# Three modulation rows moved from the output product to the class products, sums of squares put behind rows, and u's block sums put two tiles later

## The chip, the cores and the metric

The kernel runs on one core of one Trainium2 chip. The metric is the time of the whole program in device microseconds (us), as the median of several runs. A profiled execution gives, beside its own time, a trace of every instruction; positions in that trace are told in us from the first instruction.

## What is computed

One decoder block on 512 tokens of width 1024, everything in float32. A conditioning vector gives 9 x 1024 modulation values, a shift, a scale and a gate for each of three sub-layers. The sub-layers are a SwiGLU feed-forward, a token-mixing layer and a second SwiGLU; a last RMSNorm follows. What matters here, cut from the reference:

```python
mod = silu(c) @ w_ada + b_ada            # 9 x 1024: sh1, sc1, gt1, sh2, sc2, gt2, sh3, sc3, gt3
u = modulate(rmsnorm(h, g1), sh1, sc1);  h = h + 0.5 * gt1 * swiglu(u, ...)
u = modulate(rmsnorm(h, g2), sh2, sc2);  h = h + gt2 * token_mixing(u, ...)
u = modulate(rmsnorm(h, g3), sh3, sc3);  h = h + 0.5 * gt3 * swiglu(u, ...)
return rmsnorm(h, g_final)

# token_mixing: proj = u @ w_in -> p, q, k, v, gate logits
#   pooling of p, three groups of dilated window attention, merged by their softmax denominators
merged = g_pool * (y_pool @ w_pool_branch) + g_attn * (y_attn @ w_attn_branch)
return merged @ w_out
```

## The kernel before

**Products.** Activations stand feature by token, eight tiles of 128 features by 512 tokens. Each float32 operand of a product is split into a high part (ScalarE copies it to the matmul's format: `whi`, `UH`) and a low part (VectorE subtracts: `wlo`, `UL`), and each product is three matmuls, high x high, high x low, low x high (`mm3`, lines 356 to 362). Weights come by DMA in chunks of 512 KB (`raw`), are split three or four tiles ahead of their use, and stand in a ring of seven chunks.

**Modulation rows.** The 72 rows of 128 modulation values are not made on TensorE. `bg` (line 406) does one: VectorE multiplies a 128 x 1024 chunk of `w_ada` with the broadcast condition and sums along the row (line 387, one SCALAR_TENSOR_TENSOR with an accumulator). `bg_fetch` (line 422) loads the next chunks from the SyncE queue (line 379) into the tiles of `ada_free`, at most `ada_depth` rows ahead, and a chunk's tile can be loaded again only when VectorE has read it. After the eighth row of a group `ada_fin` adds the bias and, by kind, multiplies the gain in (scale) or halves (last gate).

**The mixing layer** (`mix`, line 1247). After the projections of q, k and a part of v come the attention tiles. Work on attention is put beside the projection's matmuls by hooks: `hooks(new, ...)` returns, for a tile, what is to be recorded ahead of which of its eight contraction steps k. Step 5 always carries the attention of three stages: the value products of the unit begun two tiles earlier (`at_values`, line 1138, TensorE), the transposes of the last unit, the scores of the new one, and its maximum and exponential (`at_exp`, VectorE lines 1112 and 1114, ScalarE line 1117). The four products of the values by residue class c (loop at line 1381) write one bank each; VectorE copies it to `v23` (line 1396), and the value products read `v23` in the next tile's step 5. Two tiles of gate logits follow (`gates`), with the merge of the softmax denominators (`at_merge`) and the pooling's small products.

GpSimd computes the pooling's running means in `pool_diff` (line 1205), beside the class products.

**u's block sums** (`mix_sums`, line 969) are thirteen small steps that a later blocked product of the gate logits needs: sums and differences of quarters of u on VectorE, each 128 x 1024, and their split in high and low parts. `nxt` pops the next one where a hook calls it. The names `PH`, `YL`, `YH` and `cs` are the tiles that hold them.

**The output product** (end of `merge_out`, line 1456). Tiles m = 0 to 4 of `w_out` times the merged branches, each 512 tokens wide; behind each, VectorE adds gate x product to the residual (`H`, line 1543), ScalarE squares it, and VectorE adds the square to a running sum `acc`, the lower half of tile `AR` (`sumsq`, lines 432 to 440). `bg` is called 3, 3, 2, 2 and 1 times behind the five tiles, for rows 61 to 71. Tiles 5 to 7 follow in `out_tail` (line 519), halved by tokens; in the second half of tile 6 TensorE sums `acc` over the features (`stats_t`, line 450), and the next norm starts from that. So all eight squares of the first half must have been added by then (the last three at line 557).

Each engine works through its own instructions in the order in which they were recorded; semaphores hold an instruction until its inputs are there.

## Time and profile before

| | |
|---|---|
| median of 3 runs (995.24, 996.4, 997.64) | 996.4 us |
| the profiled execution: its own time, its span in the trace | 995.25 us, 993.5 us |
| TensorE busy | 981.3 us, 99% of the span |
| VectorE busy | 787.3 us, 79% |
| ScalarE busy | 475.3 us, 48% |
| GpSimd busy | 33.9 us, 3% |
| mean granted TensorE clock | 0.999 |

In the trace's rows PE is TensorE, PEld its weight load, DVE VectorE, ACT ScalarE, POOL GpSimd and SPq the queue of SyncE, which issues the loads. A timeline row tells start, duration, engine, line, operation, output and input, shapes, and in brackets how long the engine sat idle before it and what ended that. A row of the waits tells who waited for whom: total, times, longest. A row of the windows tells, for a stretch of time, its length and then each engine's busy time and instruction count in it. Times of VectorE rows overlap a little at their ends, so what an instruction takes in a full queue is told below by the distance of two starts.

### The profile page before, as it was taken

To read this page: it belongs to the slowest core of one execution; us is meant where nothing else is said; L and a number is where in the kernel's file an instruction comes from. 1 tells how busy PE (TensorE), PEld (TensorE's weight loads), DVE (VectorE), ACT (ScalarE), POOL (GpSimd) and SP (SyncE) were. 2 spreads that over 40 slices of the span, in tenths; PEclk is the share of its full clock that TensorE was granted. 3 is DMA by queue.
4 is the path that set the end of the run, shared out by engine and by line. 5 is a ranking of instruction groups with operands and counts; after the bars stand their busy time and mean duration, and the time that the engine had idled before them with its cause. 6 is when DMAs were issued, how large, how long until landed. Compare 5 with 4: busy or idle time off the path is not lost.

```text
span 993.5 us, 16359 instructions
## 1 busy us (share of the span) xinstructions
PE 981.3 (99%) x6686; PEld 893.9 (90%) x6686; DVE 787.3 (79%) x1091; ACT 475.3 (48%) x713; POOL 33.9 (3%) x31
## 2 busy tenths in 40 slices
PE   9999999999999999999999999899999999999997
PEld 7888998989999899787879998898899899998997
DVE  7989969889797677889768877868797776676764
ACT  6453643525435453455545552455365254352553
POOL 0000000000000000007400000000000000000002
PEclk9999999999999999999999999999999999999999
DMA  9856445455563416663133336622344134241312
GB/s 348 276 196 223 149 148 178 161 191 165 181 203 106 140 56 211 213 199 120 33 118 107 107 91 201 219 64 89 103 150 135 56 110 146 85 149 43 105 45 85
DMA packets 44876, 141.74 MB, mean 143 GB/s; under 512 B 6273, under 2 KB 9089, under 8 KB 44802
## 3 DMA queue, kind: packets, MB, share of 16 engines
q1 hardware_dynamic: 44226, 140.18, 43.5%
q8 instruction: 52, 0.85, 0.3%
q10 hardware_dynamic: 576, 0.52, 0.2%
q14 instruction: 22, 0.18, 0.1%
HBM read 135.29 MB, written 2.24 MB: 138 GB/s over the span
## 4 chain that ended last, share of the span: by engine, by line
PE 83%; DVE 8%; DMA 3%; SPq 2%; ACT 2%; issue 2%; POOL 0%; POOLq 0%; DVEq 0%; ACTq 0%
PE bank L747 13%; PE bank L748 13%; PE bank L749 13%; PE bank L360 12%; PE bank L361 12%; PE bank L362 12%; DVE wlo L329 2%; SPq L1050 1%; PE bank L1710 1%; PE bank L1712 1%; PE bank L1714 1%; DMA v<-wada 1%; DMA rt<-tr 1%; DVE k L387 1%; DVE v L387 1%
## 5 line engine op out<-in xcount | busy, mean ns | idle before, releaser
L329 DVE TENSOR_TENSOR wlo<-raw,whi 128x1024 fp32r<-128x1024 f32 (+4 forms) x162 | 172.7, 1078 | 48.7 <-ACT whi L317 48.4
L747 PE MATMUL bank<-UH,whi 128*128 128x256 f32 x640 | 177.0, 276 | 0.0
L748 PE MATMUL bank<-UL,whi 128*128 128x256 f32 x640 | 176.9, 276 | 0.0
L749 PE MATMUL bank<-UH,wlo 128*128 128x256 f32 x640 | 176.9, 276 | 0.0
L317 ACT ACTIVATE whi<-raw 128x1024 fp32r<-128x1024 f32 (+4 forms) x162 | 146.1, 920 | 57.7 <-DVE raw L261 54.8
L360 PE MATMUL bank<-HI,whi 128*128 128x512 f32 (+1 forms) x406 | 146.2, 360 | 0.0
L361 PE MATMUL bank<-HK,whi 128*128 128x512 f32 (+1 forms) x406 | 145.9, 359 | 0.0
L362 PE MATMUL bank<-HI,wlo 128*128 128x512 f32 (+1 forms) x406 | 145.8, 359 | 0.0
L329 DVE TENSOR_TENSOR wlo<-X,whi 128x1024 fp32r<-128x1024 f32 (+3 forms) x104 | 111.9, 1083 | 32.2 <-ACT whi L317 31.8
L747 PEld LDWEIGHTS bank<-UH,whi 128*128 128x128 f32 x640 | 120.1, 188 | 0.4
L749 PEld LDWEIGHTS bank<-UH,wlo 128*128 128x128 f32 x640 | 120.3, 188 | 0.0
L748 PEld LDWEIGHTS bank<-UL,whi 128*128 128x128 f32 x640 | 120.2, 188 | 0.0
L747 PE MATMUL bank<-SH,whi 128*128 128x256 f32 x408 | 112.9, 277 | 0.0
L749 PE MATMUL bank<-SH,wlo 128*128 128x256 f32 x408 | 112.8, 276 | 0.0
L748 PE MATMUL bank<-SL,whi 128*128 128x256 f32 x408 | 112.8, 276 | 0.0
L317 ACT ACTIVATE whi<-X 128x1024 fp32r<-128x1024 f32 (+3 forms) x104 | 95.7, 943 | 34.3 <-DVE X L261 33.5
L360 PE MATMUL bank<-UH,whi 128*128 128x512 f32 (+1 forms) x304 | 105.7, 348 | 0.0
L361 PE MATMUL bank<-UL,whi 128*128 128x512 f32 (+1 forms) x304 | 104.3, 343 | 0.1
L362 PE MATMUL bank<-UH,wlo 128*128 128x512 f32 (+1 forms) x304 | 104.1, 342 | 0.0
L362 PEld LDWEIGHTS bank<-HI,wlo 128*128 128x128 f32 x406 | 76.2, 188 | 11.6
L360 PEld LDWEIGHTS bank<-HI,whi 128*128 128x128 f32 x406 | 76.2, 188 | 11.5
L361 PEld LDWEIGHTS bank<-HK,whi 128*128 128x128 f32 x406 | 76.3, 188 | 11.3
(345 smaller groups left out, 1841.9 us busy)
## 6 DMA issues: line engine op xcount, KB each, us to landing
raw<-wmix SPq DMA_DIRECT2D x44, 512.0 KB, 3.8
raw<-wf1i SPq DMA_DIRECT2D x31, 512.0 KB, 5.0
raw<-wf2i SPq DMA_DIRECT2D x30, 512.0 KB, 3.7
ada<-wada SPq DMA_DIRECT2D x23, 512.0 KB, 5.6
AR<-wada SPq DMA_DIRECT2D x16, 512.0 KB, 4.4
X<-wf2i SPq DMA_DIRECT2D x14, 512.0 KB, 3.7
cs<-wada SPq DMA_DIRECT2D x12, 512.0 KB, 3.7
X<-wf1i SPq DMA_DIRECT2D x12, 512.0 KB, 4.6
```

The source lines that it names most:

```text
L317: self.nc.scalar.activation(self.hi[:, y], r[:, x], AF.Copy)
L329: self.nc.vector.tensor_tensor(self.lo[:, y], r[:, x], self.hi[:, y], op=OP.subtract)
L360: M(ps, hi, uh, start=start, stop=False)
L361: M(ps, hi, ul, start=False, stop=False)
L362: M(ps, lo, uh, start=False, stop=stop)
L387: self.nc.vector.scalar_tensor_tensor(t[:, c], t[:, c], 1.0, self.cond[:, c], op0=OP.mult, op1=OP.mult, accum_out=o)
L747: M(o, hi, uh, start=start and p == 0 and k == 0, stop=False, skip_group_check=True)
L748: M(o, hi, ul, start=False, stop=False, skip_group_check=True)
L749: M(o, lo, uh, start=False, stop=k == 3, skip_group_check=True)
L1050: nc.sync.dma_start(w[32 * o:32 * o + 32], t[32 * i:32 * i + 32])
L1710: M(b, hi, self.UH[k], start=k == 0, stop=False)
L1712: M(b, hi, self.UL[k], start=False, stop=False)
```

## The change

Three things move; nothing is computed otherwise, and TensorE's and GpSimd's instructions stand in the same order as before.

- Rows 61, 62 and 63 of the modulation go from behind tiles 0 and 1 of the output product to three hooks: class product 2 at step 6, class product 3 at step 7, and the second gate tile at step 1. Their chunks are loaded one at a time into `AR`. The output product then calls `bg` 2, 2, 2, 2 and 0 times.
- In the output product the addition of a tile's square is recorded behind that tile's rows, not ahead of them.
- The block sums start two pops later: one step stays in the tile ahead of the class products, none stands in class product 0, one in class product 1, and the others in class products 2 and 3 and the gate tiles. Two steps are merged into one pop.

```diff
@@ mix_sums
-                lambda: (hi(0), whole(x[3], 4, 0)), lambda: lo(0), lambda: sub(x[3], x[3], x[1]), lambda: hi(1),
+                lambda: (hi(0), whole(x[3], 4, 0)), lambda: lo(0), lambda: (hi(1), sub(x[3], x[3], x[1])),
                 lambda: hi(2), lambda: lo(2), lambda: lo(1)], last
@@ mix
             assert self.ada_next == 61 and not self.adat, self.ada_next
+            self.ada_free, self.ada_stop, self.ada_depth = [self.AR], 64, 1
+            self.bg_fetch()
...
-            b = self.mm_tile(hooks(g23[0], [(2, lambda: by_class(1)), (3, nxt), (7, nxt)]))
+            b = self.mm_tile(hooks(g23[0], [(2, lambda: by_class(1)), (3, nxt)]))
...
+            beside = [(1, 7, nxt), (2, 2, nxt), (2, 3, clear), (2, 6, self.bg), (2, 7, nxt), (3, 2, self.at_swap), (3, 2, nxt),
+                      (3, 3, nxt), (3, 6, nxt), (3, 7, self.bg)]
             for c in range(4):
                 mid = [lambda c=c: by_class(c + 1)] if c in (1, 2) else []
-                hk = hooks(g23[c + 1], [(2, nxt), (7, nxt)] if c < 2 else [(2, clear)], mid) if c < 3 else \
-                    hooks([], [(2, self.at_swap), (2, nxt), (3, nxt), (6, nxt)])
+                hk = hooks(g23[c + 1] if c < 3 else [], [(k, f) for n, k, f in beside if n == c], mid)
...
-            gates = [self.mm_tile(hooks([], [(5, self.at_merge), (7, nxt)]))]
+            gates = [self.mm_tile(hooks([], [(2, nxt), (5, self.at_merge), (7, nxt)]))]
...
-            gates.append(self.mm_tile({1: [nxt], 3: [nxt], 6: [pool_map, lambda: self.at_fT(self.bS[1])]}))
+            gates.append(self.mm_tile({1: [self.bg, nxt], 3: [nxt], 6: [pool_map, lambda: self.at_fT(self.bS[1])]}))
@@ merge_out
-                self.sumsq(m, self.H[m])()
-                for _ in range((3, 3, 2, 2, 1)[m]):
+                add = self.sumsq(m, self.H[m])
+                for _ in range((2, 2, 2, 2, 0)[m]):
                     self.bg()
+                add()
```

What this does to VectorE's order is seen at three places. In the rows, `v_3281` is the tile `v23`, `q_3276` the tile of the fourth block sum, `uc` the low part of the first, `k_...` and `v_...` with line 387 a row's chunk; numbers of tiles differ between the two programs.

The first place is VectorE between the maxima of class product 0 and those of class product 1. Before:

```order
L1114 TENSOR_SCALAR negmax<-st 128x2
L977 TENSOR_TENSOR YL<-UH,UL 128x1024
L1396 COPY v_3281<-bank_96 128x512
L987 TENSOR_TENSOR YH<-YL,cs 128x1024
L329 TENSOR_TENSOR wlo<-raw_66,whi 128x1024
L1152 COPY q_3274<-bank_97 128x256
```

Now (the copy to `v23` is line 1400):

```order
L1114 TENSOR_SCALAR negmax<-st 128x2
L1400 COPY v_3281<-bank_96 128x512
L329 TENSOR_TENSOR wlo<-raw_66,whi 128x1024
L1152 COPY q_3274<-bank_97 128x256
L1112 ISA prob,st<-bank_90,masks 128x256
```

The block sum ahead of the copy and the one behind it are gone; the two that stood ahead of these maxima (`PH`, lines 977 and 996) are gone too.

The second place is VectorE from the last maxima to the end of class product 3. Before:

```order
L1114 TENSOR_SCALAR negmax<-st 128x2
L1396 COPY v_3281<-bank_95 128x512
L977 TENSOR_TENSOR q_3276<-UH,UL 128x1024
L985 TENSOR_TENSOR uc<-PH,k_4494 128x1024
L1152 COPY q_3274<-bank_97 128x256
L987 TENSOR_TENSOR q_3276<-q_3276,YL 128x1024
L1396 COPY v_3281<-bank_96 128x512
L329 TENSOR_TENSOR wlo<-raw_68,whi 128x1024
```

Now:

```order
L1114 TENSOR_SCALAR negmax<-st 128x2
L387 SCALAR_TENSOR_TENSOR AR,mod<-AR,cond 128x1024
L977 TENSOR_TENSOR YL<-UH,UL 128x1024
L1400 COPY v_3281<-bank_95 128x512
L987 TENSOR_TENSOR YH<-YL,cs 128x1024
L987 TENSOR_TENSOR YL<-PH,YL 128x1024
L1152 COPY q_3274<-bank_97 128x256
L977 TENSOR_TENSOR q_3276<-UH,UL 128x1024
L387 SCALAR_TENSOR_TENSOR AR,mod<-AR,cond 128x1024
L1400 COPY v_3281<-bank_96 128x512
L329 TENSOR_TENSOR wlo<-raw_68,whi 128x1024
```

Two rows and three block sums now stand in this stretch around the two copies, and two of the steps that stood here follow later. On the SyncE queue a load of `AR` stands ahead of the two small transfers of `at_swap` and another behind them.

The third place is VectorE in the output product, from the residual of tile 1 on. Before:

```order
L1543 SCALAR_TENSOR_TENSOR H<-bank_92,mod,H 128x512
L440 TENSOR_TENSOR AR<-AR,ut 128x512
L387 SCALAR_TENSOR_TENSOR k_5496,mod<-k_5496,cond 128x1024
L387 SCALAR_TENSOR_TENSOR k_5497,mod<-k_5497,cond 128x1024
L387 SCALAR_TENSOR_TENSOR v_5498,mod<-v_5498,cond 128x1024
L329 TENSOR_TENSOR wlo<-raw_67,whi 128x1024
L1543 SCALAR_TENSOR_TENSOR H<-bank_93,mod,H 128x512
L440 TENSOR_TENSOR AR<-AR,ut 128x512
```

Now:

```order
L1547 SCALAR_TENSOR_TENSOR H<-bank_92,mod,H 128x512
L387 SCALAR_TENSOR_TENSOR v_5506,mod<-v_5506,cond 128x1024
L387 SCALAR_TENSOR_TENSOR k_5504,mod<-k_5504,cond 128x1024
L440 TENSOR_TENSOR AR<-AR,ut 128x512
L329 TENSOR_TENSOR wlo<-raw_67,whi 128x1024
L1547 SCALAR_TENSOR_TENSOR H<-bank_93,mod,H 128x512
L387 SCALAR_TENSOR_TENSOR k_5505,mod<-k_5505,cond 128x1024
L387 SCALAR_TENSOR_TENSOR v_5506,mod<-v_5506,cond 128x1024
L440 TENSOR_TENSOR AR<-AR,ut 128x512
```

The addition of the square (line 440) has changed places with the rows, and one row fewer stands in this tile; behind tile 0 one row fewer stands too, and behind tile 4 none.

## The prediction

> **What bounds the kernel now.** I read the page first, then who waited for whom on TensorE, then windows and timelines around the two waits found there. The page:

> ```profile
> span 993.5 us, 16359 instructions
> PE 981.3 (99%) x6686; PEld 893.9 (90%) x6686; DVE 787.3 (79%) x1091; ACT 475.3 (48%) x713; POOL 33.9 (3%) x31
> ```

> TensorE is idle for 993.5 - 981.3 = 12.2 us in all, and its instructions are the same in the same order after the change. So the change can gain only idle time of PE. PE's waits between 440 and 660 us (total, times, longest):

> ```profile
> PE bank L450 <- DVE AR L557: 2.6, 1, 2.6
> PE bank L1147 <- DVE v L1396: 0.9, 1, 0.9
> PE bank L460 <- DVE r L455: 0.3, 1, 0.3
> ```

> The two larger ones are the places that the change touches, and both name VectorE. First the class products, as windows (length; PE, PEld, DVE, ACT, POOL busy; clock, DMA share, GB/s):

> ```profile
> 470.00:480.00 10.00, 9.24 (x70) 7.92 (x72) 9.88 (x20) 7.29 (x15) 9.63 (x7) 1.00 0.08 27
> 480.00:505.00 25.00, 25.00 (x166) 19.89 (x163) 13.85 (x32) 10.95 (x21) 2.26 (x2) 1.00 0.19 55
> ```

> VectorE is full from 470 to 480 and has 25.00 - 13.85 = 11.15 us free from 480 to 505. Its timeline ahead of the first wait, and PE's:

> ```profile
> 462.17 1.23 DVE L329 TENSOR_TENSOR wlo<-raw,whi 128x1024 fp32r<-128x1024 f32 x1 [0.44 <-ACT whi L317]
> 463.31 1.25 DVE L996 TENSOR_TENSOR PH<-PH,cs 128x1024 f32<-128x1024 f32 x1
> 464.48 2.32 DVE L329 TENSOR_TENSOR wlo<-raw,whi 128x1024 fp32r<-128x1024 f32 x1
> ...
> 468.80 1.21 DVE L977 TENSOR_TENSOR YL<-UH,UL 128x1024 f32<-128x1024 f32 x1
> 469.94 0.68 DVE L1396 COPY v<-bank 128x512 f32<-128x512 f32 x1
> ```

> ```profile
> 470.76 1.09 PE L1147 MATMUL bank<-probT,v 128*64 128x128 f32 x16 [0.90 <-DVE v L1396]
> ...
> 479.67 1.09 PE L1147 MATMUL bank<-probT,v 128*64 128x128 f32 x16
> ...
> 488.57 1.09 PE L1147 MATMUL bank<-probT,v 128*64 128x128 f32 x16
> ...
> 496.16 1.09 PE L1147 MATMUL bank<-probT,v 128*64 128x128 f32 x16
> ```

> The value products wait for a copy that stands behind block sums in VectorE's queue. Second the output product:

> ```profile
> 608.97 0.75 DVE L1543 SCALAR_TENSOR_TENSOR H<-bank,mod,H 128x512 f32<-128x512 f32 x1 [4.60 <-PE bank L362]
> ...
> 609.64 1.22 DVE L387 SCALAR_TENSOR_TENSOR k<-k,cond 128x1024 f32<-128x1024 f32 x1
> ...
> 610.78 1.22 DVE L387 SCALAR_TENSOR_TENSOR k<-k,cond 128x1024 f32<-128x1024 f32 x1
> ...
> 614.91 0.69 DVE L440 TENSOR_TENSOR AR<-AR,ut 128x512 f32<-128x512 f32 x1 [0.70 <-ACT ut L439]
> 615.52 1.22 DVE L387 SCALAR_TENSOR_TENSOR k<-k,cond 128x1024 f32<-128x1024 f32 x1
> ...
> 618.99 1.22 DVE L329 TENSOR_TENSOR wlo<-raw,whi 128x1024 fp32r<-128x1024 f32 x1
> 620.13 0.74 DVE L1543 SCALAR_TENSOR_TENSOR H<-bank,mod,H 128x512 f32<-128x512 f32 x1
> ...
> 634.75 0.48 DVE L516 SCALAR_TENSOR_TENSOR H<-bank,mod,H 128x256 f32<-128x256 f32 x1
> ...
> 640.07 0.42 DVE L557 TENSOR_TENSOR AR<-AR,gc 128x256 f32<-128x256 f32 x1
> ```

> ```profile
> 614.66 0.39 PE L362 MATMUL bank<-v,wlo 128*128 128x512 f32 x1
> ...
> 633.94 0.28 PE L362 MATMUL bank<-v,wlo 128*128 128x256 f32 x1
> ...
> 640.54 0.71 PE L450 MATMUL bank<-ones,AR 128*128 128x128 f32 x4 [2.59 <-DVE AR L557]
> ```

> The residual of tile 2 starts at 620.13 though its bank was done at 614.66 + 0.39 = 615.05: VectorE runs five us late behind the rows, and when PE comes to sum the squares, at 640.54 - 2.59 = 637.95, the last addition ends only at 640.07 + 0.42 = 640.49. Tile 0 still found VectorE waiting for PE (4.60 idle), so the lag is made here.

> **The output product.** Removed are three rows, one start-to-start distance of 1.14 each (609.64 to 610.78): 3.4 us. The additions behind the rows no longer wait for ScalarE's square, apart from tile 4's, which has no rows ahead of it:

> ```profile
> L440 DVE TENSOR_TENSOR AR<-AR,ut 128x512 f32<-128x512 f32 x4 | 2.8, 692 | 2.9 <-ACT ut L439 2.9
> ```

> So 2.9 us of idle in four waits become about 0.7. But rows now come closer to their loads: a chunk is loaded only when its tile has been read. Landing times of the `k` and of the `v` chunks (shortest, median, longest):

> ```profile
> DMA to landing us min/median/max: 3.6/5.4/7.0
> ```

> ```profile
> DMA to landing us min/median/max: 4.6/6.3/6.7
> ```

> VectorE's queue then runs so, with 0.67 for a residual (608.97 to 609.64), 0.61 for an addition (614.91 to 615.52), 1.14 for a `wlo` (618.99 to 620.13). Residual 0, rows 64 and 65, residual 1, row 66: 613.7. Row 67's tile is read at 610.8 and reloaded; before, the chunk in that place was read without a wait at 615.52, so it is there between 610.9 + 3.6 = 614.5 and 615.5. I take 615.0: a new wait of 1.3, row done at 616.1. Addition, `wlo`, residual 2: 618.6. Rows 68, 69: 620.8 (69's tile free at 613.7, landed by 620.4 at the latest). Addition, `wlo`, residual 3: 623.3. Row 70: 624.4. Row 71's tile is free at 619.7, landed at 625.1 by the median, 626.7 at the latest: done at 626.2. Its closing sums 0.4 (estimate from the rows' neighbours), addition, `wlo`, residual 4: 629.1. Tile 4's addition with its wait of 0.7: 630.4. From here to the last addition it took 640.49 - 634.75 = 5.74 before, all on VectorE: 636.1. PE asks at 637.95, so the wait of 2.59 goes, with 1.8 us to spare. With every chunk at its latest the chain is some 2.1 later, 638.2, and 0.3 of the wait stays. Taken: 2.6; ends 2.3 and 2.6. Next late is the last bank itself: done at 633.94 + 0.28 = 634.2, its addition 1.9 later.

> **The class products.** Ahead of the copy of class 0 two block sums go that cost time there: 464.48 - 463.31 = 1.17 and 469.94 - 468.80 = 1.14. (The third, `PH` from line 977, ended in a wait for ScalarE at 462.17 anyway.) The copy then starts at 467.6 and ends at 468.3; PE comes at 470.76 - 0.90 = 469.86. The 0.9 goes, and the program behind runs 0.9 earlier.

> Class 1's copy now has one block sum ahead. Where the maxima of classes 1 and 2 started, and the step behind the first:

> ```profile
> 474.61 0.41 DVE L1112 CUSTOM_DVE_ANT_0 prob<-bank,masks 128x256 f32<-128x256 f32 x1
> ...
> 477.07 1.21 DVE L987 TENSOR_TENSOR YL<-PH,YL 128x1024 f32<-128x1024 f32 x1
> ...
> 482.91 0.43 DVE L1112 CUSTOM_DVE_ANT_0 prob<-bank,masks 128x256 f32<-128x256 f32 x1 [1.18 <-PE bank L1096]
> ```

> ```profile
> 459.38 2.34 DVE L977 TENSOR_TENSOR PH<-UH,UL 128x1024 f32<-128x1024 f32 x1
> ```

> ```profile
> 463.56 2.15 POOL L1229 TENSOR_TENSOR k<-k,tr 64x512 f32<-64x512 f32 x1
> ...
> 477.21 2.39 POOL L1227 TENSOR_SCALAR k<-rt 64x496 f32<-64x496 f32 x1
> ```

> With everything 0.9 earlier the maxima start at 473.7 at the latest and end 477.07 - 474.61 = 2.46 behind that, at 476.2; a sum takes between 1.21 (477.07) and 2.34 (459.38) while GpSimd works, the copy 0.68. So the copy ends between 478.0 and 479.1, for a need at 479.67 - 0.90 = 478.77: I take no wait, since VectorE has been freed of more than 0.9 here, with 0.3 at the far end. The row at 464.48 shows why a sum can be slow: GpSimd's instruction ran until 463.56 + 2.15 = 465.71, and 465.71 + 1.09 is the 466.80 at which the `wlo` ended. [...]

> Class 2's copy gets a row and a sum ahead, 2 x 1.14. The maxima start at 482.91 - 0.90 = 482.0 and take at most 2.46 again, row 61 ends at 485.6, the sum at 486.7, the copy at 487.4; need: 488.57 - 0.90 = 487.67. Class 3's copy stands behind row 62, whose chunk is loaded when row 61 has been read. Landing of all these chunks over the program:

> ```profile
> DMA to landing us min/median/max: 3.5/4.8/7.4
> ```

> It lands by 485.6 + 4.8 = 490.4, at the latest 493.0. VectorE has done two sums, a small copy (0.6, since the 512-wide one takes 0.68) and a third sum by 491.4; the row ends at 492.6, the copy at 493.2, or at the latest at 494.8; need: 496.16 - 0.90 = 495.26. Row 63 is loaded from 492.6 on and read behind the merge, whose position is quoted below. Rows, their closing sums and the three sums put behind 480 are 3.4 + 0.4 + 3.4 = 7.2 us against 11.15 free: no cost. Without that room each us by which a copy is late costs PE one.

> On SyncE's queue the load for row 62 stands ahead of the exchange of softmax statistics:

> ```profile
> 486.46 0.33 SPq L1157 DMA_DIRECT2D scr<-st  x1
> ```

> ```profile
> 497.76 0.17 DVE L1166 TENSOR_TENSOR mm<-m,stn 128x16 f32<-128x16 f32 x1
> ```

> That load is issued at 485.6, so the exchange need not wait to be issued; and the merge reads its result eleven us behind 486.46: hidden, even behind a load of 7.4.

> **Sum.** 2.6 + 0.9 = 3.5 us. The profiled execution took 995.25, which would become 991.8; it is as low as the lowest of the three runs, 1.15 under their median of 996.4, so for a median I say 996.4 - 3.5 = 992.9.

> **Rivals.**

> Rows wait for loads. With three tiles, a row can't start sooner than a landing after the third row before it was read. If loads take 2 us more than their longest, the chain ends near 640.2, 2.2 of the wait stays, and the time is 996.4 - 0.9 - 0.4 = 995.1; with less of it, 994.4. For: rows stand closer together. Against: eight loads instead of eleven share the queue. Chance 0.13.

> [...] If class 1's sum waits for all of a 2.39 us instruction, it takes 1.2 + 2.4 = 3.6, its copy ends at 480.4, and PE waits 1.6: 994.5. For: the two instructions at 463.56 and 464.48, of which the later waited out the earlier. Against: the `YL` sum of 477.07 took 1.21 with GpSimd at work. Chance 0.09.

> The wait moves on. If the next norm, with VectorE dense behind the sums of squares, holds PE by what was gained there, only 0.9 is left: 995.5. For: the third wait, 0.3, is there. Against: that norm starts from PE's own sum and moves with it. Chance 0.08.

> Slower: the single `AR` tile. Row 62 stands ahead of class 3's copy. If its chunk lands over 7.8 us after 485.6 (495.26 less 1.14 and 0.68), PE waits one us for each further one, and all VectorE work behind it too. At twice the longest landing, 14.8, it loses 7.0: 996.4 - 3.5 + 7.0 = 999.9. Against: the longest was 7.4, and the DMA is busy for 0.19 of its time here. With other mishaps of this kind, chance 0.06.

> **Numbers.** The forecast has 0.64, the rivals the rest. The range goes from 991.4 (992.9, less the 0.3 of the third wait, less the 1.2 by which runs fall under their median) to 995.8 (the case of 995.5 with a little spread). A measurement of this kernel can tell 0.2%, 2 us, from no change: faster is under 994.4. That is most of the forecast, 0.59, and half of the late loads and of the port's case, 0.11: 0.70. Slower 0.07 (the last rival and a little of the one before), the rest 0.23.

> **What would show it.** In the changed profile PE's waits should lack line 1147 and have line 450 at most at 0.3; the fourth residual should start within 3 us of its bank; rows 67 and 71 should show idle ahead of them for their loads, about 1 us each. A wait of PE at line 1147 behind classes 1 to 3, or at line 450 of over 1 us, makes the sum wrong; so does a new wait between 645 and 660.

## The result, and the profile after

The changed kernel takes 990.61 us (median of 6 runs, 990.31 to 991.56); the kernel before, run beside it, 996.18 (6 runs, 995.07 to 997.64). The ratio is 0.9946, 95% interval 0.9933 to 0.9959: 5.6 us faster. The forecast was 3.5 us faster, 992.9 with a range from 991.4 to 995.8: the right direction, 2 us too little, and below the range. The spread shrank too, from 2.6 us to 1.25.

The profiled execution took 991.56 us. Its page, and TensorE's waits between 440 and 660 us:

```profile
span 989.8 us, 16358 instructions
PE 981.1 (99%) x6686; PEld 893.8 (90%) x6686; DVE 784.8 (79%) x1091; ACT 475.2 (48%) x713; POOL 29.7 (3%) x31
```

```profile
PE bank L460 <- DVE r L455: 0.4, 1, 0.4
```

TensorE is as busy as before (981.1 for 981.3), both waits are gone, and the third is where it was. The span lost 993.5 - 989.8 = 3.7 us, for 0.90 + 2.59 of waits. **So between the two traces the predicted sum is met, and yet the medians differ by 5.6.** The profiled execution before lay 1 us under its median (995.25 to 996.2); the one after lies 1 us above (991.56 to 990.6). What is missing should then lie in executions that were not profiled; the experiments look for it.

In the class products, VectorE has moved its work into the free stretch (length; PE, PEld, DVE, ACT, POOL busy; clock, DMA share, GB/s):

```profile
470.00:480.00 10.00, 10.00 (x82) 8.48 (x83) 7.92 (x17) 6.15 (x13) 7.88 (x7) 1.00 0.10 26
480.00:505.00 25.00, 25.00 (x157) 19.75 (x157) 21.34 (x45) 11.83 (x22) 0.00 (x0) 1.00 0.35 97
```

From 480 to 505 VectorE's busy time went from 13.85 to 21.34, the 7.5 us put there (7.2 forecast), and TensorE is full in both stretches. Its value products of classes 0 to 2, and on VectorE the four copies and the pieces beside them:

```profile
469.89 1.09 PE L1147 MATMUL bank<-probT,v 128*64 128x128 f32 x16
...
478.79 1.09 PE L1147 MATMUL bank<-probT,v 128*64 128x128 f32 x16
...
487.70 1.09 PE L1147 MATMUL bank<-probT,v 128*64 128x128 f32 x16
```

```profile
467.05 0.68 DVE L1400 COPY v<-bank 128x512 f32<-128x512 f32 x1
...
476.69 0.68 DVE L1400 COPY v<-bank 128x512 f32<-128x512 f32 x1
477.29 2.04 DVE L996 TENSOR_TENSOR PH<-PH,cs 128x1024 f32<-128x1024 f32 x1
...
486.09 0.69 DVE L1400 COPY v<-bank 128x512 f32<-128x512 f32 x1
...
490.67 1.21 DVE L387 SCALAR_TENSOR_TENSOR AR<-AR,cond 128x1024 f32<-128x1024 f32 x1
491.95 0.69 DVE L1400 COPY v<-bank 128x512 f32<-128x512 f32 x1
```

The copies end at 467.7, 477.4, 486.8 and 492.6, each 0.9 us or more before TensorE reads it. The tightest is class 2's, 0.92. Class 1's sum at 477.29 took 2.04, where the one at 486.69, with GpSimd done, took 1.22; it stands behind the copy and delays nobody.

In the output product, VectorE and then TensorE:

```profile
613.58 1.23 DVE L387 SCALAR_TENSOR_TENSOR k<-k,cond 128x1024 f32<-128x1024 f32 x1 [0.64 <-DMA k<-wada]
...
621.16 0.75 DVE L1547 SCALAR_TENSOR_TENSOR H<-bank,mod,H 128x512 f32<-128x512 f32 x1
...
622.96 1.22 DVE L387 SCALAR_TENSOR_TENSOR k<-k,cond 128x1024 f32<-128x1024 f32 x1
...
627.75 0.69 DVE L440 TENSOR_TENSOR AR<-AR,ut 128x512 f32<-128x512 f32 x1 [0.76 <-ACT ut L439]
628.36 0.48 DVE L516 SCALAR_TENSOR_TENSOR H<-bank,mod,H 128x256 f32<-128x256 f32 x1
629.69 1.29 DVE L329 TENSOR_TENSOR wlo<-raw,whi 128x512 fp32r<-128x512 f32 x2 [0.86 <-ACT whi L317]
...
634.91 0.42 DVE L557 TENSOR_TENSOR AR<-AR,gc 128x256 f32<-128x256 f32 x1
```

```profile
618.55 0.39 PE L362 MATMUL bank<-v,wlo 128*128 128x512 f32 x1
...
636.92 0.60 PE L450 MATMUL bank<-ones,AR 128*128 128x128 f32 x4
```

Row 67 (613.58) waits 0.64 for its load and row 71 (622.96) not at all. The fourth residual (621.16) starts 2.2 us behind its bank (618.55 + 0.39). The last addition ends at 634.91 + 0.42 = 635.33, TensorE comes at 636.92: 1.6 us to spare. From 628.36 on VectorE is no longer late: it waits 0.86 for ScalarE's high part of a weight.

### The profile page after: what moved, and what is told of

Same layout as the page of the kernel before. It is cut to its first block, busy times and chain, and to the rows that moved or that the text cites. A ratio compares the mean times of both kernels' runs of the same rounds, so it can differ in the third digit from the quotient of the medians.

```text
span 989.8 us, 16358 instructions
## 1 busy us (share of the span) xinstructions
PE 981.1 (99%) x6686; PEld 893.8 (90%) x6686; DVE 784.8 (79%) x1091; ACT 475.2 (48%) x713; POOL 29.7 (3%) x31
## 4 chain that ended last, share of the span: by engine, by line
PE 95%; DVE 2%; SPq 1%; issue 1%; POOL 0%; ACT 0%; DMA 0%; POOLq 0%; DVEq 0%; ACTq 0%
PE bank L360 15%; PE bank L361 15%; PE bank L362 15%; PE bank L748 13%; PE bank L747 13%; PE bank L749 13%; PE bank L1715 1%; PE bank L1719 1%; PE bank L1717 1%; SPq L1050 1%; PE bank L1394 1%; PE bank L1096 1%; PE bank L1147 1%; PE bank L1395 1%; PE bank L1396 1%
## 5 line engine op out<-in xcount | busy, mean ns | idle before, releaser
L329 DVE TENSOR_TENSOR wlo<-raw,whi 128x1024 fp32r<-128x1024 f32 (+4 forms) x162 | 170.6, 1065 | 52.8 <-ACT whi L317 52.6
L317 ACT ACTIVATE whi<-raw 128x1024 fp32r<-128x1024 f32 (+4 forms) x162 | 146.1, 920 | 57.3 <-DVE raw L261 54.5
L362 PE MATMUL bank<-HI,wlo 128*128 128x512 f32 (+1 forms) x406 | 145.8, 359 | 0.0
L329 DVE TENSOR_TENSOR wlo<-X,whi 128x1024 fp32r<-128x1024 f32 (+3 forms) x104 | 111.9, 1084 | 33.1 <-ACT whi L317 32.7
L317 ACT ACTIVATE whi<-X 128x1024 fp32r<-128x1024 f32 (+3 forms) x104 | 95.7, 943 | 33.1 <-DVE X L261 32.4
L362 PE MATMUL bank<-UH,wlo 128*128 128x512 f32 (+1 forms) x304 | 104.0, 342 | 0.0
L362 PEld LDWEIGHTS bank<-HI,wlo 128*128 128x128 f32 x406 | 76.2, 188 | 11.7
```

Source lines behind the costliest of these rows:

```text
L317: self.nc.scalar.activation(self.hi[:, y], r[:, x], AF.Copy)
L329: self.nc.vector.tensor_tensor(self.lo[:, y], r[:, x], self.hi[:, y], op=OP.subtract)
L362: M(ps, lo, uh, start=False, stop=stop)
```

## The experiments

All but the last three ran on two chips, where the kernel before had medians of 996.7 to 996.9. The last three, single profiled executions, ran on a third chip; the one execution of before timed beside them took 999.25. My theory at first (in the expectations, the two waits alike in every execution, the surplus elsewhere in the program) had as its rival that the rows' loads come at varying times, late in most executions, and hold TensorE for longer than the profile shows. A third theory, the clock, came out of the fifth run.

**The kernel before again,** with no edit.

> The kernel before, unchanged, profiled once more. Theory A (the change gains the two waits of TensorE, 0.90 and 2.59 us, in every execution alike, and the rest of the difference of the medians comes from outside the changed stretches): the waits are 0.9 and 2.6 again, each within 0.1, and what differs between executions differs at the start or the end of the program. Theory B (VectorE is saturated in both stretches before, so whatever is late in an execution goes on to TensorE, and the two waits differ from execution to execution): their sum is not 3.5 but something between 3 and 6, and moves with the time of the execution.

Measured: 996.61 us (995.17 to 997.59, 11 runs), ratio 0.9996 (0.9987 to 1.0005). Its profiled execution is again the fastest of all: 995.17, with the same two waits. So the profiled execution does not stand for the median here. It also has a wait that the first one lacks, for the low half of a weight that VectorE splits behind late rows:

```profile
630.41 0.28 PE L361 MATMUL bank<-q,whi 128*128 128x256 f32 x1
631.10 0.39 PE L362 MATMUL bank<-q,wlo 128*128 128x256 f32 x1 [0.41 <-DVE wlo L329]
```

Ahead of it TensorE's rows of this shape start 0.113 us apart, behind it 0.118, with the full clock on record. From its first value product (470.76 before, 469.73 here) to its asking at line 450 (637.95 and 637.85) TensorE takes 0.93 us longer: more than twice the wait.

**The additions behind the rows, alone.**

```diff
-                self.sumsq(m, self.H[m])()
+                add = self.sumsq(m, self.H[m])
                 for _ in range((3, 3, 2, 2, 1)[m]):
...
+                add()
```

> Only one part of the change: in the output product the additions of the squares stand behind the rows; the rows and the block sums stay where they were. VectorE loses up to 2.9 us of idle, so its chain ends at 640.5 - 2.9 = 637.6 against TensorE's 637.95. Theory A: the wait at line 450 falls from 2.6 to between 0 and 0.5, the wait at line 1147 stays at 0.9, and the time falls by 2.1 to 2.6 us. Theory B: the time falls by more than the profiled wait, 3 to 4.5 us, and its runs scatter less than those of before.

Measured: 995.28 us (993.50 to 997.83, 10 executions; an eleventh took 2551 us, and with it the median is 995.62), ratio 0.9985 (0.9974 to 0.9995). Short of both theories: the wait of 2.59 lost only 0.6. TensorE's waits, VectorE's, and a row on VectorE:

```profile
PE bank L450 <- DVE AR L557: 2.0, 1, 2.0
```

```profile
DVE k L387 <- DMA k<-wada: 2.3, 2, 1.7
```

```profile
617.01 1.23 DVE L387 SCALAR_TENSOR_TENSOR k<-k,cond 128x1024 f32<-128x1024 f32 x1 [1.73 <-DMA k<-wada]
```

The waits for ScalarE's squares went, as forecast, and rows that came earlier now wait 2.3 us for their loads: the 2.9 us of idle time changed its owner.

**The three rows, alone.**

```diff
+            self.ada_free, self.ada_stop, self.ada_depth = [self.AR], 64, 1
+            self.bg_fetch()
...
-                hk = hooks(g23[c + 1], [(2, nxt), (7, nxt)] if c < 2 else [(2, clear)], mid) if c < 3 else \
-                    hooks([], [(2, self.at_swap), (2, nxt), (3, nxt), (6, nxt)])
+                hk = hooks(g23[c + 1], [(2, nxt), (7, nxt)] if c < 2 else [(2, clear), (6, self.bg)], mid) if c < 3 else \
+                    hooks([], [(2, self.at_swap), (2, nxt), (3, nxt), (6, nxt), (7, self.bg)])
...
-                for _ in range((3, 3, 2, 2, 1)[m]):
+                for _ in range((2, 2, 2, 2, 0)[m]):
```

(The third row goes in beside `nxt` in the second gate tile.)

> Only another part: rows 61 to 63 move to the class products and gate tiles; the additions stand ahead of the rows and the block sums where they were. VectorE loses three rows, 3.4 us, in the output product. Theory A: the wait at line 450 goes, the one at line 1147 stays at 0.9, and the time falls by 2.6 us. Theory B: it falls by 3 to 4.5 us. If the rows cost something in the class products, a new wait at line 1147 behind class 2 or 3 shows it.

Measured: 992.16 us (991.51 to 993.11, 5 runs), ratio 0.995 (0.9938 to 0.9963). The output product's wait is gone from its trace, that of the class products stays (`L1147`, 0.9). It removes 2.6 us of waits and gains 4.7: most of the surplus is here.

**The block sums later, alone,** with the old rows and additions.

```diff
-                lambda: (hi(0), whole(x[3], 4, 0)), lambda: lo(0), lambda: sub(x[3], x[3], x[1]), lambda: hi(1),
+                lambda: (hi(0), whole(x[3], 4, 0)), lambda: lo(0), lambda: (hi(1), sub(x[3], x[3], x[1])),
...
+            beside = [(1, 7, nxt), (2, 2, nxt), (2, 3, clear), (2, 7, nxt), (3, 2, self.at_swap), (3, 2, nxt),
+                      (3, 3, nxt), (3, 6, nxt)]
...
-            gates = [self.mm_tile(hooks([], [(5, self.at_merge), (7, nxt)]))]
+            gates = [self.mm_tile(hooks([], [(2, nxt), (5, self.at_merge), (7, nxt)]))]
```

> Only the third part: the block sums come later; all rows and additions as before. Theory A: the wait at line 1147 goes, the one at line 450 stays at 2.6, and the time falls by 0.9 us. Theory B: it falls by 0.9 to 2 us, since GpSimd's collisions with VectorE in that stretch vary.

Measured: 995.78 us (994.02 to 998.02, 11 runs), ratio 0.9989 (0.998 to 0.9997). The wait at line 1147 is gone, that at line 450 is 2.6. The median is 1.1 us lower for the 0.9 that it removes: hardly a surplus.

**A fourth row tile,** against late loads: the kernel before, with three loads ahead in place of two.

```diff
-            self.ada_free, self.ada_stop, self.ada_depth = [ma.tile([P, D], F32, name=x) for x in ("k0", "k2", "v1")], 72, 2
+            self.ada_free, self.ada_stop, self.ada_depth = [ma.tile([P, D], F32, name=x) for x in ("k0", "k2", "v1")] + [self.cs], 72, 3
```

> The kernel before, but the rows of the output product get a fourth tile (cs, which is free there) and are loaded three ahead. Nothing else moves. Theory B, now put so: before, the rows in the output product run at the edge of their loads, so in most executions a chunk lands later than in the profiled one, VectorE waits, and TensorE's wait at line 450 is 1.5 us longer than the 2.6 of the trace; the median then falls by 1 to 2 us here, to about 995.3, its spread falls from some 3 us to 1.5, and the profiled wait stays at 2.6. Theory A (the waits are the same in every execution): the median stays at 996.9 and the spread at 3.

Measured: 996.22 us (994.52 to 997.03, 11 runs), ratio 0.9993 (0.9983 to 1.0002): loads in good time gain 0.5 us in the kernel before, not clear of nothing, and leave a spread of 2.5. Late loads as the main cause of the surplus fall; a few tenths by them are not ruled out. But this profiled execution, at 996.57, was no longer below its median, and its trace held something new behind the same wait of 2.6. Windows of TensorE alone (length, busy and instructions; granted clock; DMA share, GB/s):

```profile
638.00:640.00 2.00, 0.40 (x3) 1.00 0.68 213
640.00:642.00 2.00, 2.00 (x13) 0.63 0.71 244
642.00:644.00 2.00, 2.00 (x11) 0.52 0.38 156
644.00:646.00 2.00, 2.00 (x20) 1.00 0.04 4
```

Behind the wait TensorE's clock is at half, for 3.413 us by the clock's record, and does 11 matmuls in 2 us where it does 20 at the full clock. That costs at most 3.413 / 2 = 1.7 us (an estimate). The third theory: the wait drops the clock in most executions, not in the profiled one of before.

**The additions and the fourth tile together** (both edits above).

> The additions behind the rows, together with the fourth tile. With three tiles the additions gained 0.6 us in the trace, since 2.3 us of waits for loads took the place of 2.9 us of waits for squares. Theory B: with four tiles those waits go, VectorE's chain ends 2.9 us earlier, the wait at line 450 is under 0.5, and the median falls by 3.5 to 4.5 us, to about 992.8. Theory A: the wait goes too, but the median falls by 2.6, to 994.3.

Measured: 992.12 us (992.02 to 992.72, 5 runs), ratio 0.9954 (0.994 to 0.9968). The wait at line 450 is gone with all rows in place, the clock is full, and the time equals that of the moved rows. So the additions had failed for the loads alone, and the surplus hangs on the wait, not on how it is removed.

**The changed kernel with two row tiles, one load ahead,** which brings back a wait through late loads.

```diff
-            self.ada_free, self.ada_stop, self.ada_depth = [ma.tile([P, D], F32, name=x) for x in ("k0", "k2", "v1")], 72, 2
+            self.ada_free, self.ada_stop, self.ada_depth = [ma.tile([P, D], F32, name=x) for x in ("k0", "k2")], 72, 1
```

> The changed kernel with two tiles for the rows of the output product, loaded one ahead. Every second row waits a whole landing (3.6 to 7 us) for its tile. By the rows of the trace before, row 71 then ends near 630 and the last addition near 641, so the wait at line 450 comes back with 2 to 5 us. Theory B: the time is 2 to 5 us above the changed kernel's and its runs spread by 2.5 us or more, as before the change, since the landings now reach TensorE. Theory A: slower by the profiled wait, spread as the changed kernel's, 1.3.

Measured: 995.34 us (993.22 to 996.55, 12 runs), ratio 0.9984 (0.9975 to 0.9994); beside it **the changed kernel again**:

> The changed kernel, unchanged, on the chip of these runs. Theory B: no wait at lines 450 and 1147 above 0.3, median 5 to 6 us under that of before, spread about 1.3 us; most of the difference between its profiled execution and the others lies at the start and the end. Theory A: 3.5 us under before.

Measured: 990.79 us (990.43 to 991.85, 5 runs), ratio 0.9941 (0.9927 to 0.9956), no wait but line 460's. With two tiles the rows wait 4.5 us for loads and TensorE 2.2 at line 450; with that wait the kernel takes 995.34 - 990.79 = 4.6 us more.

**The kernel before, its wait filled:** 11 matmuls of 512 columns, into a bank that nobody reads, issued just ahead of the sums of squares. They add work of no use and start nothing earlier.

```diff
+                        for _ in range(11 if nxt == 2 else 0):
+                            nc.tensor.matmul(self.B[7], ks[0][0], ks[0][2], start=True, stop=True)
                         self.stats_t(self.B[6], A)
```

> The kernel before with eleven matmuls of 512 columns into a bank that nobody reads, ahead of the sums of squares that wait at line 450. They take about 2.5 us, so TensorE works through its wait; nothing gets earlier. Theory C: a wait of over 2 us at line 450 makes the clock gate grant half the clock for 3.4 us behind it in most executions (in the profile of the kernel with four tiles it did, in the others not), which costs 1.7 us beside the wait, and that is what the medians have and the trace of before has not. Then the median falls by 1 to 2 us, from 996.8 to about 995.2, the spread from over 3 us to 1.5, and the granted clock shows no half between start and end. Theory A (the surplus comes from start and end): median and spread stay as before.

Measured: 995.01 us (994.54 to 996.6, 11 runs), ratio 0.9988 (0.9979 to 0.9997). More work, and 1.7 us faster. The spread is 2.1, not 1.5: the profiled execution is the slowest of the eleven, 996.6, with the full clock until near its end and a wait of 0.4 at line 362, behind which the rows stay 0.113 us apart. TensorE's wait at line 450 is 0.2 instead of 2.6:

```profile
638.90 2.72 PE L544 MATMUL bank<-q,whi 128*128 128x512 f32 x11
```

```profile
PE bank L450 <- DVE AR L559: 0.2, 1, 0.2
```

**The two-tile kernel, its wait filled** with 9 such matmuls.

```diff
+                        for _ in range(9 if nxt == 2 else 0):
+                            nc.tensor.matmul(self.B[7], ks[0][0], ks[0][2], start=True, stop=True)
```

> The changed kernel with two tiles for the rows, with nine such matmuls in its wait of 2.2 us at line 450. Theory C: the median falls from 995.3 to 993.0 to 993.7, which is the changed kernel's 990.8 and the wait, and the spread from 3.3 to 1.5. Theory A: stays at 995.3.

Measured: 994.11 us (992.52 to 995.07, 11 runs), ratio 0.9975 (0.9966 to 0.9984). The direction is as expected, 1.2 us faster, but the median stays above the 993.0 to 993.7 expected and the spread shrank only from 3.3 to 2.6. Its trace has another wait, for a weight half that VectorE splits behind the rows (they waited 4.5 us for loads in the two-tile kernel), and which no filling covers:

```profile
PE bank L362 <- DVE wlo L329: 1.5, 1, 1.5
```

**The change without its additions part.**

```diff
-                add = self.sumsq(m, self.H[m])
+                self.sumsq(m, self.H[m])()
...
-                add()
```

> The change without one part: rows and block sums moved, the additions ahead of the rows as before. VectorE's chain loses the 3.4 us of the rows but keeps its 2.9 us of waits for squares. Theory C: no wait at lines 450 and 1147, so the time is the changed kernel's, 990.8 within 0.5. If the additions are worth something of their own, up to 1 us more.

Measured: 991.02 us (990.71 to 991.95, 5 runs), ratio 0.9951 (0.9936 to 0.9966), no wait but line 460's. The additions part adds nothing that can be measured once the rows are gone.

**The wait made longer:** one VectorE instruction of no use, 1.14 us, behind tile 4 in the kernel before.

```diff
+                if m == 4:
+                    v.tensor_tensor(self.cs, self.cs, self.cond, op=OP.mult)
```

> The kernel before with one more instruction of 1.14 us on VectorE behind tile 4 of the output product (a product whose result nobody reads). The wait at line 450 becomes 3.7 us, longer than the 3.4 us for which the gate was seen at half clock. Theory C: the gate falls in every execution, so no run is under 997.8, the profile shows half the clock for 3.4 us behind the wait, and the median is 1.1 to 2 us above before's. Theory A: every run 1.1 us later, the lowest near 995.9, and the profile shows no half clock or shows it by chance.

Measured: 999.49 us (997.99 to 999.59, 7 runs), ratio 1.0026 (1.0016 to 1.0037): 2.8 us for 1.1 us more of a wait, where 1.1 to 2 were expected. The wait and the windows:

```profile
PE bank L450 <- DVE AR L557: 3.7, 1, 3.7
```

```profile
640.00:642.00 2.00, 0.01 (x1) 0.80 0.76 176
642.00:644.00 2.00, 2.00 (x9) 0.50 0.87 272
644.00:646.00 2.00, 2.00 (x12) 0.50 0.52 209
646.00:648.00 2.00, 2.00 (x11) 0.50 0.00 0
648.00:650.00 2.00, 2.00 (x19) 0.99 0.49 68
```

Half the clock here for twice 3.413 us, part of the first still inside the wait.

**The unchanged kernel before, three more profiled executions,** to see the drop on the very kernel that the forecast was made from.

> The kernel before, unchanged, one more profiled execution. Theory C: if its time is near 995, the granted clock is full from start to end as in the two executions profiled so far; if it is 996.4 or more, the clock shows 0.5 for 3.4 us or a multiple behind the wait at line 450, which is 2.6 us in both cases. Theory A: the longer time is at the start or the end.

> As the one before: the kernel before, unchanged, another profiled execution; near 995 with the full clock, 996.4 or more with 0.5 for 3.4 us behind the wait at line 450 (theory C), or longer elsewhere (theory A).

> As the two before: the kernel before, unchanged, a third further profiled execution; near 995 with the full clock, 996.4 or more with 0.5 for 3.4 us behind the wait at line 450 (theory C), or longer elsewhere (theory A).

Measured: 995.29 with the full clock, 997.06 and 996.70 with half of it for 3.413 us behind the wait, which is 2.8, 2.6 and 2.8 in the three. The windows of the one of 997.06, and TensorE around the wait:

```profile
640.00:642.00 2.00, 1.25 (x8) 0.85 0.64 240
642.00:644.00 2.00, 2.00 (x12) 0.50 0.73 258
644.00:646.00 2.00, 2.00 (x16) 0.79 0.00 0
646.00:648.00 2.00, 2.00 (x20) 1.00 0.34 53
```

```profile
640.75 0.71 PE L450 MATMUL bank<-ones,AR 128*128 128x128 f32 x4 [2.57 <-DVE AR L557]
...
644.61 0.38 PE L361 MATMUL bank<-q,whi 128*128 128x256 f32 x1
644.82 0.28 PE L362 MATMUL bank<-q,wlo 128*128 128x256 f32 x1
```

And the windows of the profiled execution that the forecast was made from:

```profile
638.00:640.00 2.00, 0.00 (x0) 1.00 0.83 242
640.00:642.00 2.00, 1.46 (x12) 1.00 0.72 219
642.00:644.00 2.00, 2.00 (x20) 1.00 0.67 270
```

The same kernel, the same wait, and then the full clock. The price can be read from the traces: from the end of the wait to TensorE's second matmul behind line 460 (a row of line 361) it is 640.54 to 643.74 here, 3.20 us, and 640.75 to 645.51 in the one of 997.06, 4.76: 1.6 us. The other two traces with a drop behind a wait of this length, that of 996.70 and that of the fourth tile, have 4.79 and 4.78.

In the ten traces with a wait of this kind, which of the two comes goes with when the wait falls. In the records the clock changes only on a grid of 3.413 us: the full clock lasts 986.452 us in the trace of before and 979.625 in that of the changed kernel, 289 and 287 steps of 3.4133. The grid does not start with the program: these two stretches begin 4.98 and 6.43 us behind the first instruction. What parts the two cases is how much idle time one step holds. Worked out from the clock's records and TensorE's rows of the ten profiled executions with a wait of 2 us or more at line 450 (the most in one step, 3.413 us each):

```
idle us in one step of 3.413     clock behind it
1.33  1.44  1.55  1.82  1.87  1.91   full
2.18  2.51  2.57  2.94               half
```

So waits of 2.6 to 2.8 us, shorter than a step, went with a drop where one step held 2.18 us of idle time or more; with 1.91 or less there was none in these traces. What happens between the two figures is not shown.

The mean granted clock is also listed for every execution that was only timed. Half a clock for 3.413 of 995 us lowers it by 0.0017, so I take an execution at 0.997 or less as one with a drop. The 17 profiled ones bear that out: the four with a drop in their records show 0.996 and 0.997, the others 0.998 or 0.999. (The wait is that of the kernel's profiled execution.)

```
kernel                                 wait L450   executions at 0.997 or less
changed (both sets), rows alone,
  change without additions,
  additions with a fourth tile           none        0 of 26
before, wait filled                      0.2         0 of 11
two-tile kernel, wait filled             none        0 of 11
additions alone                          2.0         4 of 10
changed, two tiles                       2.2         8 of 12
block sums alone                         2.6         6 of 11
before with a fourth tile                2.6         9 of 11
before (again)                           2.6         8 of 11
before (beside the experiments)          2.6        59 of 74
before, wait longer                      3.7         7 of 7
```

In the 74 executions of before, the 59 have a median of 997.02 us and the other 15 of 995.55. Six of the 59 show 0.996 or 0.995, at 997.7 to 999.25 us, and may hold more than one step.

Two things here are not explained by one wait of fixed length. Were its place on the grid random, a wait of 2.6 us would put more than 1.91 into one step in at most (3.413 + 2.6 - 2 x 1.91) / 3.413 = 0.64 of the executions (an estimate from the figures above); 59 of 74 are 0.80. And with the additions alone the four executions with a drop have a median of 997.3, the six without 994.5: 2.8 us apart, where one drop costs 1.6. So in executions that were not profiled the wait may well be longer; no run shows its length there.

## Why the prediction was right in direction and short in size

**What held.** Both waits went. Copies 0 to 3 were put at 468.3, 478.0 to 479.1, 487.4 and 493.2; they ended at 467.7, 477.4, 486.8 and 492.6, each some 0.6 earlier. The rows, put into free VectorE time and between SyncE's transfers, cost nothing. The time in the trace, 3.7 against 3.5, is right.

**What held by luck** is the place of the last addition: put at 636.1, less the 0.9 gained earlier, 635.2, it came at 635.33. Two errors cancelled there. Tile 4's addition was put at 630.4 - 0.9 = 629.5 and ended at 628.44, 1.1 earlier, since the rows hardly waited for loads. From the next residual (628.36) to the end the forecast carried over the 5.74 of a late VectorE; it took 6.97, since VectorE, no longer late, waited for ScalarE and TensorE there. The wait goes either way.

**What failed** is one step in the paragraph of the sum: the profiled execution lay "1.15 under their median of 996.4, so for a median I say 996.4 - 3.5". That took the 1.15 for scatter that the change leaves alone. Most of it was part of the wait's price. Behind a wait of 2.6 us the clock also falls to half for 3.413 us in most executions (59 of 74, by their mean clock), at 997.02 - 995.55 = 1.5 us by the medians of the two groups, 1.6 in the traces; the profiled execution was one of the few without. So the term "2.6" for the output product was mis-sized: for the median the wait with its drop was worth about 4. Rows alone, which removes it, gained 4.7; the two-tile kernel, which brings 2.2 of it back, lost 4.6. The range's low end, 991.4, had the same fault: it allowed for the third wait and for scatter, and nothing for a price beyond the two waits' lengths.

**What stays open.** From 996.84, the median of the 74, to 990.79 are 6.05 us. Of that 3.5 are the waits themselves, and 996.84 - 995.55 = 1.3 the share of the clock in the median. The last 1.25 us are not placed. They seem to go with the output product's wait, since rows alone has 0.8 of them (995.55 - 2.6 = 992.95 by the executions without a drop, 992.16 measured) while adding the block sums to that gains 1.1 for its wait of 0.9. Some profiled executions of before and its variants have a further wait of 0.4 at line 362 for a late weight half, and in the one of before again it cost 0.93 with the slower rows behind it, which may be a part; longer waits in executions that were not profiled may be another. None of the runs isolates them. Executions also differ for a reason that has nothing to do with the change: between 114 and 154 us TensorE's rows stand 0.118 apart instead of 0.113 for some 27 us in five of the 17 traces (the first of before, two of the later three, the filled wait, the first of the changed kernel), at a full clock on record, and that stretch is 1.05 us longer in them.

**The rivals.** Rows waiting for loads: 0.64 us for one row, none of it on TensorE's path; the rival comes true with two tiles and with the additions alone. GpSimd slowing class 1's sum (the case of 994.5, the "port's case" of the chances): no run shows a port, only times. The slow sum was there, but behind the copy: 2.04 us from 477.29, where GpSimd's instruction of 476.94 (1.31) ran until 478.25, and 478.25 + 1.09 is 479.34, the end of the sum within 0.01. In the other direction GpSimd gained, below. The wait moving on: line 460 went from 0.3 to 0.4, nothing more. The single `AR` tile: row 62 ended at 490.67 + 1.21 = 491.88, 0.7 ahead of its forecast, and no copy was late. The exchange of statistics was indeed hidden: its 16 KB, issued 0.5 us behind the 512 KB load (485.06 and 485.60), took 3.4 us to land instead of 1.4 (before, then after, both from 480 to 500 us), and its result is read some 11 us after the issue.

```profile
scr<-st SPq DMA_DIRECT2D x1, 16.0 KB, 1.4
```

```profile
scr<-st SPq DMA_DIRECT2D x1, 16.0 KB, 3.4
```

**Signs named ahead.** Line 1147 is gone and line 450 at nothing; the fourth residual is 2.2 us behind its bank (within 3). Idle ahead of row 67 was 0.64 for the 1.3 worked out, ahead of row 71 none for about 1: row 67's chunk was there 3.6 us after its tile had been read, for the 4.2 taken, row 71's within 4.6, for the median of 5.4.

## What to carry to other kernels

A wait of TensorE may cost more than its length, here one of 2.6 to 2.8 us by another 1.6 where the clock fell to half behind it: look at the granted clock in the windows just behind it, in more than one profiled execution, and price the drop as well. Where the profiled execution lies at the edge of the runs' spread, ask what it lacks, and compare the mean clock of the timed executions with its own, before its distance from the median is carried over as a constant. And where a wait behind one engine is removed, check what that engine then meets next: the additions alone only swapped ScalarE's squares for DMA landings.

## What the runs showed of the hardware that was not expected

```profile
L1227 POOL TENSOR_SCALAR k<-rt 64x496 f32<-64x496 f32 x4 | 9.4, 2348 | 0.3
```

```profile
L1227 POOL TENSOR_SCALAR k<-rt 64x496 f32<-64x496 f32 x4 | 6.7, 1677 | 0.3
```
